# The means' column in a buffer of the "nm" tag: the arrays behind it lie 32 bytes lower in SBUF

## The chip, the cores and the metric

The kernel runs on one core of one Trainium2 chip. The metric is the device time of one execution in microseconds (us); times below are medians over runs unless one run is named.

## What is computed

A decoder trunk of two layers over 256 tokens of width 2048, in float32. Layer 0 mixes with a gated short convolution, layer 1 with multi-head latent attention (16 heads); each layer has a squared-ReLU MLP with 8192 hidden columns, and each of the four sub-layers ends in a DeepNorm LayerNorm.

```python
def sq_relu_mlp(x, w1, w2):
    return jnp.square(jax.nn.relu(x @ w1)) @ w2

for layer in range(DEPTH):                      # DEPTH = 2
    if layer < N_A:                             # layer 0
        mix = short_conv_mixer(h, conv_w_in[layer], conv_w[layer], conv_w_out[layer])
    else:                                       # layer 1
        k_nope, k_pe, v = shared_latent_kv(h, ...)
        mix = mla_mixer(h, ..., k_nope, k_pe, v, cos, sin)
    h = layer_norm(ALPHA * h + mix, ln_g[layer, 0], ln_b[layer, 0])
    h = layer_norm(ALPHA * h + sq_relu_mlp(h, mlp_w1[layer], mlp_w2[layer]),
                   ln_g[layer, 1], ln_b[layer, 1])
```

## The kernel before

Every product is formed from float32 operands that are split into a rounded part ("hi") and the rest ("lo"), so one product takes three matmuls: hi with hi, hi with lo, lo with hi. ScalarE (ACT) casts hi, VectorE (DVE) subtracts to get lo. Weights stream in from HBM as 128x1024 blocks on the SyncE queue (`raw` or `w` tiles), are split into a ring of eight `hi`/`lo` pairs, and are used by TensorE (PE) at once. Activations stay in SBUF.

The work has these stages in order of time: the convolution mixer (products `ps_u`), the first MLP, the latent projections and the attention (`ps_k`, `ps_q`, `ps_v`, `ps_p`, `S`, `tp`, `po`), the output projection (`ps_u` again) and the second MLP. The two MLPs are the larger part of the time. In an MLP, `mlp()` writes out a list of operations with costs and dependencies, and `Work.arrange` places them in one fixed order by a small simulation; the instructions are then issued in that order. In this list two kinds of PE work alternate:

- a *chunk* of the up-projection: 16 matmuls of 512 moving columns (`ps_m<-xhl,hi`), then 16 of 256 (`ps_m<-xhl,lo`);
- a *group* of the down-projection, in a seven-product form for 2x2 blocks: 7 products of three matmuls with 512 moving columns each, summed in the PSUM tiles `sum`. The three matmuls are those of `dot`: the stationary operand is a 128x128 block of the hidden activations (`hc`, `ha`), the moving operand a 512-column half of a weight tile: hi, then lo, then hi again.

Of the seven products of a group the sixth takes its weights from a tile of its own, called `t4`: 128 partitions, its hi part 2048 bytes wide and its lo part behind it. The other six read the ring of `hi`/`lo` tiles.

```python
    FAST = (("1", "11", "11"), ("3", "S4", "22"), ("5", "S1", "T1"), ("6", "S2", "T2"),
            ("2", "12", "21"), ("4", "22", "T4"), ("7", "S3", "T3"))
...
                def fourth():
                    box["f"] = fast.tile([P, 2, BW], F32R, tag="t4", name="t4", bufs=1)
                    scalar.copy(box["f"][:, 0, :], b11())
```

SBUF tiles come from pools, which lie one behind another in each partition: `const`, `act`, `raws`, `whl` (the ring), `tmp`, `small`, and behind these whatever pool is open for a stage: `fast` during an MLP (two `sf` tiles of 4096 bytes and `t4`), `att` and within it `att2` during the attention. `small` holds narrow columns (means, variances, scales); each buffer of a tag takes 32 bytes there. `Norm.means` makes the column `off` (the negative means of the tokens, scaled) at the end of the first MLP; it is read by eight DVE instructions that add up the down-projection's blocks.

In the profile nearly every instruction has the line L71, that of the recording helper, so groups are told apart by the tiles' names. Numbers in names are left out, so `t4` shows as `t`, which is also the name of a 256-column scratch tile; MATMULs on `t` with 512 columns are those on `t4`.

Of the kernel before, what the change touches and what calls it, by code (L numbers as in the profile page):

```python
# [10 lines left out]
F32 = mybir.dt.float32  # L11
# [5 lines left out]
P = 128  # L17
# [36 lines left out]
def trunk(ctx: ExitStack, tc: tile.TileContext, opening, xT, vecs, w_in, w_out, w_kv, w_q, w_uk, w_uv,  # L54
# [32 lines left out]
    small = ctx.enter_context(tc.tile_pool(name="small", bufs=2))  # L87
# [140 lines left out]
    def psum(name):  # L228
        return Banks.next().tile([P, 512], F32, tag="mm", name=name)
# [146 lines left out]
    class Norm:  # L376
# [10 lines left out]
        def means(self):  # L387

            ps = psum("mu0c")
            for t in range(2):  # L390
                tensor.matmul(ps[:, t:t + 1], xres[:, 0, t * P:(t + 1) * P], ones[:, 0:1], start=True, stop=True)
            self.off = small.tile([P, 2], F32, tag="off", name="off", bufs=1)
            vector.tensor_scalar(self.off, ps[:, 0:2], -self.scale, None, ALU.mult)

        def prepare(self, m):
# [1058 lines left out]
```

## Time and profile before

| | |
|---|---|
| median of 3 runs | 1997.64 us (1997.62 to 1998.24) |
| profiled execution: device time | 1998.73 us |
| profiled execution: span, first to last instruction | 1996.9 us |
| TensorE clock granted | 0.998 |
| PE busy | 1983.1 us (99%), 11058 matmuls |
| PE weight loads busy | 1735.0 us (87%) |
| DVE busy | 1752.6 us (88%) |
| ACT busy | 1388.6 us (70%) |
| DMA queue q1, share of 16 engines | 61.5% |
| chain that ended last | PE 98%, DVE 1% |

The profiled execution's span is 1.8 us shorter than its device time, and its device time is 1.1 us above the median of the runs. Rows of groups give: line, engine, operation, written tile `<-` read tiles, shapes, count, busy time in us, mean duration of one in ns, and idle time of the engine ahead of them. A matmul's duration overlaps that of the next one, so the cost of a matmul in a stream is the distance from its start to the next start, which is less than its duration.

### The profile page before, as it was taken

The page shows a single profiled execution, that of the slowest core. Times are in us where ns is not written, and L with a number is a line of the kernel's source. Part 1 is how long each engine was busy: PE and PEld are TensorE (multiplying, and loading weights), DVE is VectorE, ACT ScalarE, POOL GpSimd, SP SyncE. Part 2 cuts the span into 40 slices and gives each one's busy share as a digit, 9 for nine tenths or more (in the row PEclk, how much of TensorE's full clock was granted, in tenths as well). Part 3 has the DMA queues.
Part 4 walks back from the last instruction along what each step waited for, and adds up shares of the span by engine and source line. Part 5 has one row for each costly group of instructions (what it writes and reads, how often), then busy time and mean ns, then how long its engine had stood idle before and what let it go on. Part 6 is the DMA issues. An engine that isn't in the chain of part 4 may idle for free.

```text
span 1996.9 us, 29770 instructions
## 1 busy us (share of the span) xinstructions
PE 1983.1 (99%) x11058; PEld 1735.0 (87%) x11058; DVE 1752.6 (88%) x2630; ACT 1388.6 (70%) x2069; POOL 2.3 (0%) x21
## 2 busy tenths in 40 slices
PE   9999999999999999999999999999999999999997
PEld 8888888988888888888889998898888888888886
DVE  7667667689999999999988888878999999999997
ACT  6444445577887888878856655567788788887871
POOL 0000000000000000000000000000000000000000
PEclk9999999999999999999999999999999999999999
DMA  9755556456666666666765543644666666666673
GB/s 341 230 188 189 191 186 188 156 164 195 208 200 202 205 202 205 200 202 207 221 208 158 165 129 117 204 163 154 201 203 206 200 203 204 202 206 202 199 248 110
DMA packets 107858, 387.39 MB, mean 194 GB/s; under 512 B 11969, under 2 KB 12737, under 8 KB 107713
## 3 DMA queue, kind: packets, MB, share of 16 engines
q1 hardware_dynamic: 107568, 385.36, 61.5%
q8 instruction: 86, 1.41, 0.3%
q14 instruction: 60, 0.48, 0.1%
q10 hardware_dynamic: 144, 0.13, 0.0%
HBM read 383.35 MB, written 2.10 MB: 193 GB/s over the span
## 4 chain that ended last, share of the span: by engine, by line
PE 98%; DVE 1%; issue 0%; ACT 0%; DVEq 0%
PE ps_m L71 31%; PE sum L71 27%; PE ps_u L71 20%; PE ps_d L71 4%; PE ps_w L71 4%; PE ps_g L71 4%; PE ps_q L71 1%; PE ps_v L71 1%; PE S L71 1%; PE ps_k L71 1%; PE ps_wo L71 1%; PE po L71 1%; PE ps_p L71 1%; PE turned L71 0%; DVE lo L71 0%
## 5 line engine op out<-in xcount | busy, mean ns | idle before, releaser
L71 DVE TENSOR_TENSOR lo<-w,hi 128x1024 fp32r<-128x1024 f32 x536 | 640.8, 1220 | 38.5 <-ACT hi L71 37.7
L71 ACT CAST hi<-w 128x1024 fp32r<-128x1024 f32 x536 | 541.8, 1061 | 64.2 <-DVE w L71 63.3
L71 ACT CAST hi<-raw 128x1024 fp32r<-128x1024 f32 x278 | 289.9, 1051 | 252.9 <-PE ps_u L71 155.0
L71 DVE TENSOR_TENSOR lo<-raw,hi 128x1024 fp32r<-128x1024 f32 x278 | 333.8, 1221 | 112.3 <-ACT hi L71 39.7
L71 PE MATMUL ps_m<-xhl,hi 128*128 128x512 f32 x1792 | 425.6, 390 | 0.0
L71 PEld LDWEIGHTS ps_m<-xhl,hi 128*128 128x128 f32 x1792 | 336.1, 188 | 71.7
L71 PE MATMUL sum<-hi,hc 128*128 128x512 f32 x736 | 278.0, 391 | 0.0
L71 PE MATMUL sum<-lo,hc 128*128 128x512 f32 x656 | 257.3, 392 | 0.0
L71 PE MATMUL sum<-hi,ha 128*128 128x512 f32 x640 | 246.5, 389 | 0.0
L71 PEld LDWEIGHTS ps_m<-xhl,lo 128*128 128x128 f32 x1792 | 229.8, 191 | 8.7
L71 PE MATMUL ps_m<-xhl,lo 128*128 128x256 f32 x1792 | 232.5, 283 | 0.0
L71 DVE TENSOR_TENSOR w<-w,w 128x512 f32<-128x512 f32 x312 | 213.7, 685 | 0.3
L71 PE MATMUL ps_u<-xhl_a,hi 128*128 128x512 f32 x704 | 168.1, 391 | 0.0
L71 PEld LDWEIGHTS sum<-hi,hc 128*128 128x128 f32 x736 | 138.6, 188 | 26.7 <-DVE t L71 0.3
L71 PEld LDWEIGHTS ps_u<-xhl_a,hi 128*128 128x128 f32 x704 | 129.4, 188 | 25.1
L71 PEld LDWEIGHTS sum<-hi,ha 128*128 128x128 f32 x640 | 120.2, 188 | 26.2
L71 PEld LDWEIGHTS sum<-lo,hc 128*128 128x128 f32 x656 | 123.6, 188 | 22.3
L71 ACT COPY sums<-sum 128x512 f32<-128x512 f32 x194 | 112.8, 596 | 12.3 <-PE sum L71 11.8
L71 ACT COPY t<-ps_m 128x256 f32<-128x256 f32 x112 | 42.4, 378 | 97.9 <-PE ps_m L71 97.9
L71 ACT COPY sum<-sums 128x512 f32<-128x512 f32 x174 | 105.4, 606 | 0.8
L71 PE MATMUL ps_w<-xd,hi 128*128 128x258 f32 x512 | 94.4, 284 | 0.5 <-DVE xres L71 0.5
L71 PEld LDWEIGHTS ps_u<-xhl_a,lo 128*128 128x128 f32 x704 | 90.3, 191 | 3.4
(201 smaller groups left out, 2785.4 us busy)
## 6 DMA issues: line engine op xcount, KB each, us to landing
w<-in_w_dram SPq DMA_DIRECT2D x224, 512.0 KB, 3.8
w<-in_w2f_dram SPq DMA_DIRECT2D x208, 512.0 KB, 4.3
raw<-in_w_in_dram SPq DMA_DIRECT2D x88, 512.0 KB, 4.5
raw<-in_w_dram SPq DMA_DIRECT2D x64, 512.0 KB, 4.4
raw<-in_w_out_dram SPq DMA_DIRECT2D x32, 512.0 KB, 4.2
raw<-in_w_o_dram SPq DMA_DIRECT2D x32, 512.0 KB, 3.7
raw<-in_w2f_dram SPq DMA_DIRECT2D x16, 512.0 KB, 4.6
row<-in_opening_dram SPq DMA_DIRECT2D x15, 384.0 KB, 5.0
```

Source lines behind the costliest of these rows:

```text
L71: ins = op(*args, **named)
```

## The change

The column `off` had a tag of its own with one buffer. It now takes the next buffer of the tag `nm`, which has two buffers and is otherwise used by the LayerNorm statistics.

```diff
             ps = psum("mu0c")
             for t in range(2):
                 tensor.matmul(ps[:, t:t + 1], xres[:, 0, t * P:(t + 1) * P], ones[:, 0:1], start=True, stop=True)
-            self.off = small.tile([P, 2], F32, tag="off", name="off", bufs=1)
+            self.off = small.tile([P, 2], F32, tag="nm", name="off")
             vector.tensor_scalar(self.off, ps[:, 0:2], -self.scale, None, ALU.mult)
```

In the built programs all five engines have the same instructions in the same order with the same waits; no instruction is added, removed or moved. What differs is where tiles lie. The pool `small` is 32 bytes shorter, so the tags behind `off` in it and the pools opened behind it start 32 bytes lower. Everything up to `tmp` (activations, raw weights, the `hi`/`lo` ring, all of which start at multiples of 128) stays where it was. Start of each tile in its partition, in bytes:

| tile (pool) | before | remainder by 64 | after | remainder by 64 |
|---|---|---|---|---|
| `sf`, two buffers (fast) | 216736, 220832 | 32 | 216704, 220800 | 0 |
| `t4` (fast) | 224928 | 32 | 224896 | 0 |
| `kpe` (att) | 216736 | 32 | 216704 | 0 |
| `rk` (att) | 218816 | 0 | 218784 | 32 |
| `mask_t` (att) | 219904 | 0 | 219872 | 32 |
| `pt`, two buffers (att2) | 221440, 222976 | 0 | 221408, 222944 | 32 |

## The prediction

> **What bounds the kernel now.** I read the page first. Its rows for the span, for PE, and for the chain of waits (by engine, then by line):
>
> ```profile
> span 1996.9 us, 29770 instructions
> PE 1983.1 (99%) x11058; PEld 1735.0 (87%) x11058; DVE 1752.6 (88%) x2630; ACT 1388.6 (70%) x2069; POOL 2.3 (0%) x21
> PE 98%; DVE 1%; issue 0%; ACT 0%; DVEq 0%
> PE ps_m L71 31%; PE sum L71 27%; PE ps_u L71 20%; PE ps_d L71 4%; PE ps_w L71 4%; PE ps_g L71 4%; PE ps_q L71 1%; PE ps_v L71 1%; PE S L71 1%; PE ps_k L71 1%; PE ps_wo L71 1%; PE po L71 1%; PE ps_p L71 1%; PE turned L71 0%; DVE lo L71 0%
> ```
>
> The end is set by the matmul stream itself; most of the chain is `ps_m` and `sum`, the two kinds of MLP work. So a change that moves only addresses can gain or lose in two ways: if a matmul's own spacing depends on where its operands lie, or if DVE becomes so slow that PE waits for it. For the second I read the windows view in the middle of each MLP (busy us and count by engine PE, PEld, DVE, ACT, POOL, then clock and DMA):
>
> ```profile
> 600.00:700.00 100.00, 100.00 (x509) 85.21 (x508) 97.27 (x128) 80.37 (x111) 0.00 (x0) 1.00 0.68 205
> 1600.00:1700.00 100.00, 100.00 (x516) 85.56 (x515) 96.72 (x127) 83.09 (x120) 0.00 (x0) 1.00 0.66 203
> ```
>
> PE never pauses there; DVE has 2.7 to 3.3 us of each 100 to spare.
>
> For the first way I asked which matmuls read a tile that moves. In the MLPs it is `t4` alone (`sf` is read by ACT and DVE only). The view of the tile `sum` gives duration in ns as min/median/max:
>
> ```profile
> L71 PE MATMUL sum<-hi,hc x736: 387/389/504, 411.3 to 1921.5; 128*128 128x512 f32 x184
> L71 PE MATMUL sum<-lo,hc x656: 389/389/402, 411.5 to 1921.7; 128*128 128x512 f32 x164
> L71 PE MATMUL sum<-hi,ha x640: 389/389/397, 445.1 to 1921.9; 128*128 128x512 f32 x160
> L71 PE MATMUL sum<-t,hc x216: 393/397/399, 447.8 to 1921.0; 128*128 128x512 f32 x108
> L71 PE MATMUL sum<-t,ha x96: 397/397/398, 489.8 to 1921.2; 128*128 128x512 f32 x96
> ```
>
> These are matmuls of one shape with stationary operands from the same two arrays. Those whose moving operand lies in the ring take 389 ns; those that read `t4` take 397, with hardly any spread: the fastest `t4` matmul (393) is slower than the median of the others. Now one group in detail. The groups view, first from 704.9 to 707.1 us (products 3 to 5 of this group and the edges), then from 707.1 to 708.3 (the `t4` product and the one behind it; count, busy us and mean ns of one):
>
> ```profile
> L71 PE MATMUL sum<-lo,hc 128*128 128x512 f32 x4 | 1.6, 390 | 0.0
> L71 PE MATMUL sum<-hi,ha 128*128 128x512 f32 x4 | 1.6, 389 | 0.0
> L71 PE MATMUL sum<-hi,hc 128*128 128x512 f32 x3 | 1.2, 389 | 0.0
> ```
>
> ```profile
> L71 PE MATMUL sum<-t,hc 128*128 128x512 f32 x2 | 0.6, 396 | 0.0
> L71 PE MATMUL sum<-t,ha 128*128 128x512 f32 x1 | 0.4, 397 | 0.0
> L71 PE MATMUL sum<-hi,hc 128*128 128x512 f32 x1 | 0.4, 392 | 0.0
> L71 PE MATMUL sum<-lo,hc 128*128 128x512 f32 x1 | 0.4, 398 | 0.0
> L71 PE MATMUL sum<-hi,ha 128*128 128x512 f32 x1 | 0.4, 389 | 0.0
> ```
>
> Behind `t4` the stream does not fall back to 389 at once, although the ring is read again. The next chunk's first two matmuls are still above it (the same view from 708.60 to 708.75, which holds the first, from 708.72 to 708.95, which holds both, and from 709.2 to 711, where it is steady):
>
> ```profile
> L71 PE MATMUL ps_m<-xhl,hi 128*128 128x512 f32 x1 | 0.4, 395 | 0.0
> L71 PE MATMUL ps_m<-xhl,hi 128*128 128x512 f32 x2 | 0.6, 394 | 0.0
> L71 PE MATMUL ps_m<-xhl,hi 128*128 128x512 f32 x9 | 2.2, 389 | 0.0
> ```
>
> The durations overlap, so I look whether the excess is also in the spacing. Timeline of the same group (start, length, what), its first four matmuls and the later ones that I use:
>
> ```profile
> 703.72 0.40 PE L71 MATMUL sum<-hi,hc 128*128 128x512 f32 x1
> 703.95 0.40 PE L71 MATMUL sum<-lo,hc 128*128 128x512 f32 x1
> 704.19 0.39 PE L71 MATMUL sum<-hi,ha 128*128 128x512 f32 x1
> 704.42 0.40 PE L71 MATMUL sum<-hi,hc 128*128 128x512 f32 x1
> ...
> 705.11 0.39 PE L71 MATMUL sum<-hi,hc 128*128 128x512 f32 x1
> ...
> 707.15 0.63 PE L71 MATMUL sum<-t,hc 128*128 128x512 f32 x2
> ...
> 707.85 0.39 PE L71 MATMUL sum<-hi,hc 128*128 128x512 f32 x1
> ...
> 708.54 3.80 PE L71 MATMUL ps_m<-xhl,hi 128*128 128x512 f32 x16
> ```
>
> From 705.11 to 707.15 are nine spacings: 2.04 us, 226.7 ns each. From 707.15 to 708.54 are six: 1.39 us, where six steady ones take 1.36. So the excess is real time on PE, about 30 ns by these rounded starts up to the group's end, and it goes on into the chunk.
>
> **The change part by part.**
>
> *The instructions.* None is added, removed or moved. The column takes the second `nm` buffer, which nothing has used until then; the next norm's statistics go to the first, and only those after the attention come back to this one, long after the column's last reader. Cost: nothing, on both sides.
>
> *`t4`, 32 past a multiple of 64 before, a multiple after.* What sets its matmuls apart from their neighbours? Not shape, order (hi, lo, hi as everywhere) or PSUM. No wait either: the rows above show no idle time, and a wait would scatter where these spread over 6 ns. It is written by an ACT cast and a DVE subtraction as the ring is. What is left is the place: `t4` is the only moving operand of 512 columns that begins 32 past a multiple of 64; all the ring's halves begin at multiples of 128, as `t4` will. I take it that the start within 64 bytes costs the time. The trace shows no such tile at another place, so this is inferred by elimination, not shown.
>
> The price by the rows: the three `t4` matmuls cost 7 + 7 + 8 = 22 ns over 389, the five behind them 3 + 9 + 0 + 6 + 4 = 22 (the 4 is 393, from 394 as the mean of 395 and 393). Together 44 ns a group; with the medians of all groups (three times 8 in the first part) 46. There are (216 + 96) / 3 = 104 such groups, so 104 x 46 ns = 4.8 us. All of it lies on PE, which is 100% busy in these stretches.
>
> Bounds: nothing, if the place is not the cause; 104 x 24 ns = 2.5 us, if only the three reads get cheap and the unrest behind them has another cause; 4.8 us if both go. I take 4.8, since the unrest starts only at `t4` and the nine spacings ahead of it are even.
>
> *Does DVE let PE have it?* PE would run 46 ns faster per group. A group and its chunk are 21 + 32 = 53 matmuls, so 100 us hold 516 / 53 = 9.7 of them, and PE gains 0.45 us in 100. DVE's 2.7 us to spare cover that six times.
>
> *The attention.* `kpe` goes to a multiple of 64, the two `pt` leave it; both are moving operands of unsplit float32 matmuls, 32 of 128 and 32 of 256 columns each. Groups view with shapes kept apart:
>
> ```profile
> L71 PE MATMUL S<-kqva 128*128 128x256 f32 x32 | 9.6, 380 | 0.0
> L71 PE MATMUL S<-kpe,kqva 128*128 128x256 f32 x32 | 9.5, 379 | 0.0
> L71 PE MATMUL S<-kpe,kqva 128*128 128x128 f32 x32 | 6.4, 283 | 0.4 <-DVE kqva L71 0.4
> L71 PE MATMUL S<-kqva 128*128 128x128 f32 x32 | 6.2, 273 | 0.0
> ```
>
> At 256 columns `kpe`, 32 off now, costs no more than the aligned operand (379 against 380); at 128 columns 10 ns more. So `kpe` may win 32 x 10 ns = 0.3 us and `pt` lose as much: net 0. At worst `pt` pays 46 / 3 = 15 ns on 64 matmuls, 1.0 us; at best `kpe` wins 0.6 (64 x 10 ns) and `pt` loses nothing.
>
> *DVE and ACT on the moved tiles.* Operations of one shape, first with the moved tile, then without:
>
> ```profile
> L71 DVE TENSOR_TENSOR t<-w,t 128x512 fp32r<-128x512 f32 x104 | 71.2, 685 | 0.0
> L71 DVE TENSOR_TENSOR w<-w,w 128x512 f32<-128x512 f32 x312 | 213.7, 685 | 0.3
> L71 DVE TENSOR_TENSOR ha<-sf,hc 128x1024 fp32r<-128x1024 f32 x48 | 58.5, 1218 | 0.0
> L71 DVE TENSOR_TENSOR lo<-w,hi 128x1024 fp32r<-128x1024 f32 x536 | 640.8, 1220 | 38.5 <-ACT hi L71 37.7
> L71 DVE TENSOR_TENSOR sf<-ps_m,t 128x256 f32<-128x256 f32 x112 | 46.8, 418 | 0.1
> ```
>
> 685 and 685, 1218 and 1220: DVE does not notice the place. `rk` and `mask_t`, which lose their multiple of 64, are read by DVE only. I put all this at nothing.
>
> *The sum.* The profiled execution took 1998.73 us with a span of 1996.9; less 4.8 they would be 1993.9 and 1992.1. The median of the runs is 1.1 us lower than the profiled time, so the forecast is 1997.64 - 4.8 = 1992.8 us, 0.24% less.
>
> **The rivals.** I call a change of over 0.2% (4.0 us) faster or slower, about what a measurement of this kernel can tell from no change.
>
> *No change: the place is not the cause.* Then 397 belongs to something that stays with `t4`, such as being read soon after it is written, and the time stays at 1997.6. For it: the trace has no second tile to compare, and `kpe` at the same remainder costs nothing at 256 columns. Against it: `kpe` is read by unsplit matmuls, which take 380 ns for half the columns, so a slower fetch could hide behind the slower columns; and freshness should make a wait or scatter, and there is neither. [...] Chance 0.16.
>
> *Half: the reads get cheap, the unrest stays,* or PE meets an operation that comes a little later than it does: 1997.64 - 2.5 = 1995.1. Against it: the even spacings ahead of `t4`. For it: the group's first matmuls start 230 to 240 ns apart too (703.72 to 704.42), with no `t4` near, behind 256-column matmuls. Chance 0.08.
>
> *Slower: DVE pays for the new place.* Once `sf` and `t4` start at the same remainder as the ring and the raw weights, DVE instructions that read two such tiles might collide. About 1,070 us (104 groups at 9.7 in 100 us) hold at least 71.2 + 58.5 + 46.8 = 176 us of DVE work on these tiles, and 3% of 1,070, or 32 us, to spare. PE starts to wait when that work grows by 32 / 176 = 18%; at 21% and no gain from `t4` the time is 1997.6 + 5 = 2002.6. Against it: `lo<-w,hi` reads two tiles at multiples of 128 already, at 1220 ns. Chance 0.04, with the other cases that end over 4.0 us slower.
>
> **How the numbers follow.** The forecast keeps 0.72: 1992.8, between 1991.8 (4.8 and the 0.6 of `kpe` gained, and 0.4 to 0.6 by which runs differ) and 1993.8 (`pt` at its worst). The half case lies at 1995.1 and with the same spread ends at 1995.6. From 1991.8 to 1995.6 are 0.72 + 0.08 = 0.80, which is the range; no change (0.16) and slower (0.04) are left out. Faster by over 4.0 us is the forecast without its weak edge, 0.71; within 0.2% are no change, the half case and that edge, 0.25; slower 0.04.
>
> **What would show it.** Right: all `sum<-t` matmuls at 389 instead of 397, the two `sum` matmuls behind them and the next chunk's first two at 389; the group from its first start to the chunk's first start 4.82 us before (703.72 to 708.54), 4.78 after; span 1992.1. The unrest in the first two products stays, as the ring does not move. Half: `sum<-t` near 389 but 398 behind it. Wrong: `sum<-t` still 397 at the new place, then the place was never the cause; or `sum<-t` at 389 and the span unchanged, with idle time of PE ahead of `hi` or `lo` in the MLP windows. A `po<-pt` row 10 ns or more longer would show the price at the attention.

## The result and the profile after

The changed kernel takes 1993.77 us (median of 13 runs, 1993.14 to 1994.14) against 1998.06 us for the kernel before in the same comparisons: ratio 0.9978, 95% interval 0.9971 to 0.9986, so 4.3 us or 0.22% faster. Forecast were 1992.8 us and 0.24%. The profiled execution's span went from 1996.9 to 1991.9 us. The page of the changed kernel, its rows for the span and the engines:

```profile
span 1991.9 us, 29770 instructions
PE 1978.0 (99%) x11058; PEld 1734.5 (87%) x11058; DVE 1752.0 (88%) x2630; ACT 1388.2 (70%) x2069; POOL 2.3 (0%) x21
```

PE is busy 5.1 us less, DVE and ACT by less than 1 us: the gain is in the matmul stream. The view of the tile `sum` (duration ns min/median/max):

```profile
L71 PE MATMUL sum<-hi,hc x736: 389/389/501, 410.7 to 1916.4; 128*128 128x512 f32 x184
L71 PE MATMUL sum<-lo,hc x656: 389/389/398, 410.9 to 1916.7; 128*128 128x512 f32 x164
L71 PE MATMUL sum<-hi,ha x640: 389/389/397, 444.4 to 1916.9; 128*128 128x512 f32 x160
L71 PE MATMUL sum<-t,hc x216: 389/389/389, 447.1 to 1916.0; 128*128 128x512 f32 x108
L71 PE MATMUL sum<-t,ha x96: 388/389/389, 488.9 to 1916.2; 128*128 128x512 f32 x96
```

The matmuls on `t4` are at 389 ns like the rest, where they were at 397. The timeline of the group that was shown before, now from 702.17:

```profile
702.17 0.40 PE L71 MATMUL sum<-hi,hc 128*128 128x512 f32 x1
...
705.60 0.61 PE L71 MATMUL sum<-t,hc 128*128 128x512 f32 x2
...
706.96 3.79 PE L71 MATMUL ps_m<-xhl,hi 128*128 128x512 f32 x16
710.58 1.60 PE L71 MATMUL ps_m<-xhl,lo 128*128 128x256 f32 x12
```

From `t4` to the next chunk are 1.36 us for six spacings, 226.7 ns each; before it was 1.39. The unrest behind `t4` is gone with its cause. The group takes 4.79 us from its first start to the chunk's, against 4.82.

One thing is new. In the waits of PE's weight loads a row stands that the kernel before did not have (us in total, times, longest):

```profile
PEld sum L71 <- ACT sum L71: 0.8, 2, 0.4
```

Once in each MLP a weight load now waits for ACT, 0.4 us each time, which copies a stored sum back into PSUM.

To compare kernels below I work out two numbers from each trace's matmul starts, over the 104 groups: by how much the spacings of the three `t4` matmuls exceed three times 226.7 ns, and the same for the eight matmuls behind them. Before these were 22 and 25 ns, now 0 and 0 in the median group. Where a text below says "shift", it means how many bytes further, modulo 256, the moving operand starts than the weights of the same matmul.

### The profile page after: what moved, and what is told of

Same layout as the page of the kernel before. It is cut to its first block, busy times and chain, and to the rows that moved or that the text cites. A ratio compares the mean times of both kernels' runs of the same rounds, so it can differ in the third digit from the quotient of the medians.

```text
span 1991.9 us, 29770 instructions
## 1 busy us (share of the span) xinstructions
PE 1978.0 (99%) x11058; PEld 1734.5 (87%) x11058; DVE 1752.0 (88%) x2630; ACT 1388.2 (70%) x2069; POOL 2.3 (0%) x21
## 4 chain that ended last, share of the span: by engine, by line
PE 98%; DVE 1%; issue 0%; ACT 0%; DVEq 0%
PE ps_m L71 31%; PE sum L71 27%; PE ps_u L71 20%; PE ps_d L71 4%; PE ps_w L71 4%; PE ps_g L71 4%; PE ps_q L71 1%; PE ps_v L71 1%; PE S L71 1%; PE ps_k L71 1%; PE ps_wo L71 1%; PE po L71 1%; PE ps_p L71 1%; PE turned L71 0%; DVE lo L71 0%
## 5 line engine op out<-in xcount | busy, mean ns | idle before, releaser
L71 ACT ACTIVATE sf<-sf 128x512 f32<-128x512 f32 x120 | 76.6, 638 | 27.4 <-DVE sf L71 27.3
```

Of the source, the lines that this page charges most:

```text
L71: ins = op(*args, **named)
```

## The experiments

**Is it `t4` alone, and is it the multiple of 64?** Two kernels move `t4` and nothing else, one from the kernel before, one from the changed one:

```diff
-                    box["f"] = fast.tile([P, 2, BW], F32R, tag="t4", name="t4", bufs=1)
+                    box["f"] = fast.tile([P, 2 * BW + 32], F32R, tag="t4", name="t4", bufs=1)[:, 8:8 + 2 * BW].rearrange("p (v c) -> p v c", v=2)
```

> The kernel before with t4 alone begun 32 bytes later (224960, a multiple of 64 but not of 128); sf, kpe, pt and all else stay where they were. Theory (the start of t4 within 64 bytes costs the time): all t4 matmuls at 389 ns, the two sum matmuls and two ps_m matmuls behind them at 389, time 4.3 us below the kernel before, as the change had. Rival (another moved tile brings the gain, sf or those of the attention): t4 matmuls may get cheap but the time stays within 1 us of before. Rival (a multiple of 128 is needed): t4 matmuls stay at 397 and the time at that of before.

> The changed kernel with t4 alone put back to 224928 (32 past a multiple of 64); sf and the attention's tiles stay at their new places. Theory: t4 matmuls at 397 again, the unrest behind them back, time equal to the kernel before within 0.5 us. Rival (another moved tile brings the gain): time stays within 1 us of the changed kernel, 4.3 us below before.

With `t4` put back to its old place in the changed kernel: 1997.74 us against 1997.72 before (ratio 1.0, 0.9991 to 1.0009). So the whole gain is `t4`'s; `sf` and the attention's tiles give nothing that can be seen (0.02 us between the two). But `t4` at 224960, a multiple of 64, made the kernel before slower: 2000.4 us (ratio 1.0014, 1.0005 to 1.0023). The view of `sum`, its `t4` rows, first for `t4` put back, then for `t4` at 224960:

```profile
L71 PE MATMUL sum<-t,hc x216: 393/397/399, 447.4 to 1920.8; 128*128 128x512 f32 x108
L71 PE MATMUL sum<-t,ha x96: 397/397/397, 489.4 to 1921.1; 128*128 128x512 f32 x96
```

```profile
L71 PE MATMUL sum<-t,hc x216: 394/397/398, 446.8 to 1922.6; 128*128 128x512 f32 x108
L71 PE MATMUL sum<-t,ha x96: 394/394/394, 488.8 to 1922.8; 128*128 128x512 f32 x96
```

The `t4` matmuls themselves cost about the same (397 ns at the old place, 394 to 397 at 224960); the unrest behind them grew from 25 to 50 ns and reaches the tenth matmul behind (the eight counted above hold 40 of the 50). Over 104 groups that is the measured 2.7 us. The rule that the prediction inferred, a start within 64 bytes, is wrong.

**Which places are free?** From the changed kernel, `t4` at other offsets, a different one in each MLP (the first number in the slice above becomes `16 if idx == 1 else 4` and so on, in elements of four bytes):

> The changed kernel with t4 at 64 past a multiple of 128 in the first MLP and at 16 past it in the second. Theory (2048 bytes that begin inside a stretch of 64 bytes touch 33 such stretches instead of 32): first MLP 389 ns, second MLP 397, as at 32. Rival (stretches of 128 bytes): 397 in both. Rival (only an odd multiple of 32 costs): 389 in both. Rival (lines of 16 bytes): 389 in both, since 16 is a line's start.

> The changed kernel with t4 at 4 bytes past a multiple of 64 in the first MLP and at 48 past it in the second. Theory (stretches of 64 bytes): 397 ns in both, however small the shift. Rival (only an odd multiple of 32 costs): 389 in both. Rival (lines of 16 bytes): above 389 at 4, 389 at 48. Rival (cost grows with the shift): 4 nearer to 389, 48 above 397.

The two kernels took 1999.79 and 1999.35 us (one run each). Every one of these places costs, and not in the order of a growing shift: in the table below 16 costs the least in the product itself (10 ns) and 4 the most (29 ns). The theory falls with 64 (23 ns where it had none), whole lines of 16 bytes with 16 (10 ns, and 40 behind it); of the rivals that of 128 bytes is left. I then noticed that in the changed kernel the operands of `ps_m`, `ps_u` and `sum`, moving or stationary, all start 128 past a multiple of 256, which left two theories: a moving operand must begin at such a multiple itself (A), or it must lie where the weights lie that are loaded beside it (B). Four kernels for that:

```text
 e5: hi part of t4 at its place and lo part 32 bytes off in the first MLP; hi part 32 and lo part 64 bytes off in the second
 e6 (from the kernel before):  + shim pool of 32 bytes ahead of the ring's pool
 e7 (from the changed kernel): + shim pool of 32 bytes ahead of the pool act
 e8: t4 at +128 bytes in the first MLP, +256 in the second
```

The shim is one small tile that is cleared once. In e6 what lies behind the ring moves with it, so `t4` goes to 64. In the second MLP of e5 the kernel is not what was meant: its lo slice begins at element `BW + 16` of the tile, so the lo part did not stay at its place but went to a shift of 64.

> The changed kernel with t4's two parts placed apart: in the first MLP the hi part (read by matmuls 1 and 3 of the product) at its changed place and the lo part (matmul 2) 32 bytes further, in the second MLP hi 32 bytes further and lo at its changed place. The theory of 64-byte stretches has fallen (t4 at 64 past a multiple of 128 cost more than at 32). If each read pays for its own place: first MLP about 9 ns in matmul 2 alone and 389 ns in 1 and 3; second MLP 9 ns each in 1 and 3. If a read off the others' place disturbs a rhythm between the moving reads and the weight loads beside them: spacings above 227 ns go on for five or more matmuls behind a single odd read, so the first MLP's group loses 20 ns or more for one read.

> The kernel before with 32 bytes put in ahead of the ring of hi and lo tiles, so the ring begins 32 past a multiple of 128 and t4 at 64 past; activations (xhl, hc, ha, z) stay at multiples of 128. Theory A (a moving operand must itself begin at a multiple of 128): every sum matmul with a moving operand in the ring pays about 7 ns (some 2,500 with those of ps_d and ps_v, 18 us), ps_m, whose moving operand is xhl and whose weights are the ring, stays at 389; time about 2016. Theory B (what counts is where the moving operand lies relative to the weights that are loaded beside it): ps_m and ps_u pay too, some 5,500 matmuls of 512 columns at 7 ns, 38 us; time about 2036.

> The changed kernel with 32 bytes put in ahead of all activations, raw weights, ring and fast tiles: every operand of every large matmul lies 32 past a multiple of 128, and all of them keep their places relative to each other. Theory A (absolute start): all 5,900 matmuls of 512 columns pay about 7 ns, 41 us, and those of 256 columns up to as much; time 2035 to 2060. Theory B (relative places): nothing changes, sum, ps_m and t4 matmuls at 389, time within 0.5 us of the changed kernel, 1993.8.

> The changed kernel with t4 128 bytes further in the first MLP and 256 bytes further in the second (everything else, and with it the weights hc and ha, at 128 past a multiple of 512, as t4 was in the changed kernel). If what counts is the place modulo 128: 389 ns in both. Modulo 256: above 389 in the first, 389 in the second. Modulo 512: above 389 in both.

With everything 32 bytes off, but together, the time is 1993.82 us (ratio to before 0.9979, 0.997 to 0.9989), that of the changed kernel. With the ring and what lies behind it 32 bytes off against the activations it is 2020.75 us (ratio 1.0114, 1.0097 to 1.0131). Groups view with shapes kept apart, two of the wide rows for everything together, then for the ring's kernel:

```profile
L71 PE MATMUL ps_m<-xhl,hi 128*128 128x512 f32 x1792 | 424.6, 390 | 0.0
L71 PE MATMUL ps_u<-z,hi 128*128 128x512 f32 x256 | 61.2, 391 | 0.0
```

```profile
L71 PE MATMUL ps_m<-xhl,hi 128*128 128x512 f32 x1792 | 437.0, 396 | 0.0
L71 PE MATMUL ps_u<-z,hi 128*128 128x512 f32 x256 | 62.3, 396 | 0.0
```

In the ring's kernel the moving operands of `ps_m` (`xhl`) lie where they always did; only their weights moved, and their wide matmuls still pay 6 ns. So A is out: with everything moved together no operand's own place cost anything (1993.82 us against 1993.77), and with the ring and what lies behind it moved against the activations 22.8 us were lost (2020.75 against 1998.0), so what counts here is where the moving operand lies relative to the weights. (B's size, 38 us, was too large: the narrow matmuls of `ps_m` and `ps_u` became 1 to 3 ns cheaper at this shift, 280 to 282 by duration against 283, and the first five wide ones of a `ps_u` chunk had been dear already, spaced by 233, 236, 228, 232 and 231 ns in the kernel before.) The trace of `t4` at +128 and +256, groups view over the first MLP, then over the second:

```profile
L71 PE MATMUL sum<-t,hc 128*128 128x512 f32 x108 | 33.2, 391 | 0.0
L71 PE MATMUL sum<-t,ha 128*128 128x512 f32 x48 | 19.1, 398 | 0.0
```

```profile
L71 PE MATMUL sum<-t,hc 128*128 128x512 f32 x105 | 32.1, 389 | 0.0
L71 PE MATMUL sum<-t,ha 128*128 128x512 f32 x48 | 18.7, 389 | 0.0
```

At 256 bytes it is free again (389 ns), at 128 not (391 and 398). The kernels e5 and e8 took 1997.08 and 1995.58 us (one run each). All places of `t4` together, as its shift against the weights `hc` and `ha` modulo 256, with the excess worked out from the starts (median or mean of about 52 groups each):

| shift of `t4`, bytes | three `t4` matmuls, ns | the eight behind, ns | kernel |
|---|---|---|---|
| 0 (also +256) | 0 | 0 | changed, e8 |
| 4 | 29 | 38 | e4 |
| 16 | 10 | 40 | e3 |
| 32 | 22 | 25 | before, e2 |
| 48 | 20 | 36 | e4 |
| 64 | 23 | 40 | e1, e3 |
| 128 | 16 | 25 | e8 |
| hi 0, lo 32 | 15 | 38 | e5 |
| hi 32, lo 64 | 21 | 2 | e5 |

At 16 and 64 the unrest goes on past the eight, to 50 ns in all, and at 48 to 40. Summed over the 16 spacings from `t4` on, the excess of all groups is 4.84 us before and 7.57 in e1, 6.88 in e3, 6.53 in e4, 3.94 in e5 and 2.39 in e8; the differences from before are those of the measured times within 0.1 us, in the kernels with one run too.

One odd read (lo alone at 32) unsettles the stream for ten matmuls, its own included, and costs 53 ns; three odd reads (32, 64, 32) cost 21 and leave 2 ns behind. So what is lost is not a fixed price for each read. That spacings above 227 ns go on behind a single odd read is what e5 was to tell; the rhythm between moving reads and weight loads, from which its expectation derived this, was the author's guess and is not shown.

**Does the shift set a steady spacing?** In a chunk all wide and narrow matmuls have one shift. Two kernels give five stages shifts of their own, by starting the arrays `xhl_a`, `z`, `xhl` and `oT` some bytes into their room:

```diff
-        t = act.tile([P, ROOM[tag] // 4], dtype, tag=tag, name=name)[:, :n]
+        t = act.tile([P, ROOM[tag] // 4], dtype, tag=tag, name=name)[:, at // 4:at // 4 + n]
```

> The changed kernel with the moving operands of five stages shifted against the weights that are loaded beside them, by a number of bytes of its own in each: the convolution's inputs 64 (ps_u from xhl_a), its outputs z 96, the first MLP's xhl 128, the attention's output oT 160, the second MLP's xhl 192. Theory B (place relative to the weights, modulo 256): each of these 512-column matmuls is spaced by more than the 226.7 ns at 0, by 4 to 9 ns; at 128 the cost of t4 at 128 (about 8 ns at first) stays for the whole chunk; in all some 3,850 matmuls by about 7 ns, 27 us. Rival (a moving operand pays only when it differs from the moving operand ahead of it): no cost inside a chunk at any shift, since all its reads are shifted alike, and the time stays within 2 us of the changed kernel. If a shift gives less than 226.7 ns, a kernel faster than the changed one is at hand.

> The same with other shifts: xhl_a 16, z 224, the first MLP's xhl 4, oT 32, the second MLP's xhl 240. Theory B: oT at 32 and z at 224 (32 to the other side) near the 233.5 ns that a shift of the ring by 32 gave; 4, 16 and 240 tell how near to 0 the place must be: if whole lines of 16 bytes count, 4 costs nothing and 16 something; if every byte counts, 4 costs too. Rival as before: no cost inside a chunk at any shift.

They took 1997.79 and 2013.01 us (one run each). From the starts, mean spacing in the settled part of a chunk and the whole chunk of 32 matmuls:

| stage | shift, bytes | wide, ns | narrow, ns | chunk, ns |
|---|---|---|---|---|
| `ps_u` (`xhl_a`) | 0 | 227 | 120 | 5571 |
| `ps_u` (`xhl_a`) | 16 | 232 | 117 | 5576 |
| `ps_u` (`xhl_a`) | 64 | 229 | 113 or 118, by turns | 5519 |
| `ps_u` (`oT`) | 32 | 233 | 117 | 5600 |
| `ps_u` (`z`) | 96 | 233 | 120 | 5653 |
| `ps_u` (`oT`) | 160 | 234 | 119 | 5640 |
| `ps_u` (`z`) | 224 | 233 | 118 | 5627 |
| `ps_m` | 0 | 227 | 120 | 5541 |
| `ps_m` | 4 | 240 | 124 | 5797 |
| `ps_m` | 128 | 233 | 119 | 5626 |
| `ps_m` | 192 | 233 | 113 | 5558 |
| `ps_m` | 240 | 233 | 117 | 5612 |

The groups view over the first MLP shows the extreme, first with `ps_m` at 0 (changed kernel), then at 4 (second of the two kernels):

```profile
L71 PE MATMUL ps_m<-xhl,hi 128*128 128x512 f32 x857 | 203.1, 389 | 0.0
```

```profile
L71 PE MATMUL ps_m<-xhl,hi 128*128 128x512 f32 x832 | 207.8, 401 | 0.0
```

The shift costs inside chunks where all moving reads are shifted alike (wide matmuls at 229 to 240 ns against 227), so the rival falls: it is not the step from one moving operand to the next. `z` at 224, 32 bytes below its weights, gives 5627 ns; the ring 32 bytes above `z` gave 5627 too, although there the weights moved. Of the shifts tried zero is best for the wide matmuls (227 ns), but not for the narrow ones (120 ns, against 113 at 192), and at 64 the whole chunk of `ps_u` is 52 ns shorter than at zero. That is also why the first of the two kernels lies only 4 us above the changed one instead of 27: from the starts, its shifted wide matmuls cost 14 us more in all, its narrow ones 9 us less. In the second, the shift of 4 alone makes 56 chunks x 256 ns = 14 us. The chunks of the convolution at 64 take turns between 5490 and 5543 ns, with narrow matmuls at 113 and at 118.

**A version that beats both.** First I tried to give each kind its best shift: the lo weights, which only narrow matmuls of these chunks load, were moved alone (64 bytes, or 192 in the later stages; the rope tables went to the attention's pool for room).

> The changed kernel with the lo weight tiles alone moved against the moving operands, in the products of 16 wide and 16 narrow matmuls only (ps_u and ps_m): the narrow matmuls (256 columns) read the lo weights, the wide ones (512) the hi weights, which stay at 0. The lo weights lie 64 bytes further in the convolution and the first MLP, 192 bytes further in the output projection and the second MLP; in all other products they stay at 0. Room comes from the rope tables, which move into the attention's pool. Theory B, with the shifts' measured spacings: wide matmuls keep 226.7 ns, narrow ones go from 120 to 113 or 114, about 16 x 6 = 96 ns a chunk; some 185 chunks, less what the change of place costs at each turn between wide and narrow (0 to 25 ns): time 13 to 18 us below the changed kernel, 1976 to 1981. Rival (the spacing depends on the place of the moving operand alone, as a shift of it moved it against everything): narrow matmuls stay at 120 and the time at 1993.8. If DVE, at 97% in the MLPs, cannot keep up with a PE that is 1% faster, PE waits ahead of hi and lo and less is gained.

It takes 1991.05 us (ratio to before 0.9966, 0.9954 to 0.9978), 2.7 us less than the changed kernel instead of 13 to 18: the narrow matmuls settle at 118 ns, not at 113, and the groups of the second MLP, which come behind them, take 35 ns more each. With the shift alone their spacing is not given: behind wide matmuls at 0 they settle at 118 ns, behind wide ones at their own shift of 64 or 192 they had 113, in the convolution by turns with 118. So the last kernel takes the shift of 64 as it was measured, for moving operands of wide and narrow matmuls together, in all five stages (`at=64` in the lines above):

> The changed kernel with the moving operands of ps_u and ps_m (xhl_a, z, the two MLPs' xhl, oT) 64 bytes further, weights where they were: the shift that gave the convolution's chunks 5519 ns instead of 5571 (16 wide matmuls at 229.5 ns, 16 narrow at 115). Theory B: the same chunk in all five stages; 73 chunks of ps_u gain 52 ns each (3.8 us), 112 chunks of ps_m between 22 ns (5541 before, 5519) and 50 ns (with the unrest ahead of them), 2.5 to 5.6 us: time 1984.4 to 1987.5. Rival (the gain belongs to the convolution's place in time or to its arrays): ps_m stays near 5541 ns a chunk and the time at 1991 to 1994.

It takes 1985.23 us, ratio to before 0.9936 (0.9923 to 0.995): 0.64% less than the kernel before, 8.5 us less than the changed one, inside what was expected. Groups view over the first MLP (440 to 985 us) of this kernel, then of the kernel before:

```profile
L71 PE MATMUL ps_m<-xhl,hi 128*128 128x512 f32 x864 | 207.6, 392 | 0.0
L71 PE MATMUL ps_m<-xhl,lo 128*128 128x256 f32 x855 | 106.0, 276 | 0.0
L71 PE MATMUL sum<-t,hc 128*128 128x512 f32 x108 | 32.9, 389 | 0.0
```

```profile
L71 PE MATMUL ps_m<-xhl,hi 128*128 128x512 f32 x850 | 202.0, 390 | 0.0
L71 PE MATMUL ps_m<-xhl,lo 128*128 128x256 f32 x848 | 110.0, 283 | 0.0
L71 PE MATMUL sum<-t,hc 128*128 128x512 f32 x108 | 33.6, 396 | 0.0
```

By duration wide matmuls are 2 ns dearer, narrow ones 7 ns cheaper. By the distance of their starts, against the changed kernel, wide ones of `ps_m` are 3.3 ns dearer and narrow ones 5.9 cheaper, so a chunk takes 5499 ns instead of 5541: 112 of them make 4.7 us, and 73 of `ps_u` at about 50 ns 3.7 us, together 8.4 of the 8.5 us.

## Why the prediction was right, and where not

*Which matmuls pay, and how much.* Right. The excess of 22 ns in the `t4` product and of 22 to 25 behind it vanished: from the starts, the eight spacings from `t4` on held 4.85 us above 226.7 ns each over all groups before, as the sum had it, and 0.58 us after.

*Both parts go together.* Right, and `t4` put back brings both back (22 and 25 ns). The half rival's first clause, an unrest with another cause, is out.

*DVE lets PE have it.* Right for DVE, which stays at 97.6 and 96.5 us of each 100 in the middle of the MLPs, but the sum lacked a term. In two groups PE waits for ACT's copy into PSUM, the row of waits shown above; in the first the spacings behind `t4` are 390 and 336 ns where 227 is normal, in the second 383 and 339, 0.27 us each. That is 0.5 of the 0.58 us left, the half rival's second clause, and takes 4.8 to the measured 4.3 us. That the faster stream brings these waits on is not shown: the kernel with `t4` put back, as slow as before, has one of 0.5 us in its trace. The forecast's 1992.8 was low by that and by the kernel before running at 1998.06 in the later runs. The span of 1991.9 (1992.1 forecast) agrees better than it should, since the first `sum` matmul already starts 0.6 us earlier (410.7 against 411.3), ahead of any `t4`.

*DVE and ACT on the moved tiles.* Right. ACT's 120 activations of `sf` take 638 ns, 640 before, and its casts from `sf` of 1024 columns 1066, 1068 before. DVE in the groups view after:

```profile
L71 DVE TENSOR_TENSOR t<-w,t 128x512 fp32r<-128x512 f32 x104 | 71.0, 683 | 0.0
L71 DVE TENSOR_TENSOR ha<-sf,hc 128x1024 fp32r<-128x1024 f32 x48 | 58.4, 1217 | 0.0
L71 DVE TENSOR_TENSOR sf<-ps_m,t 128x256 f32<-128x256 f32 x112 | 46.6, 416 | 0.4 <-ACT t L71 0.2
```

*The attention.* Net nothing, as said, but by another way. Neither `kpe` gained its 10 ns nor `pt` lost them; rows after:

```profile
L71 PE MATMUL S<-kpe,kqva 128*128 128x128 f32 x32 | 6.5, 283 | 0.4 <-DVE kqva L71 0.4
L71 PE MATMUL po<-pt,kqva 128*128 128x128 f32 x32 | 6.1, 274 | 0.0
```

283 is what `kpe` had before, so those 10 ns are not the place's; 274 is what `pt` had before.

*The mechanism.* The step that failed, with no harm to the number, is "the start within 64 bytes costs the time". The runs show in its place: what counts is the shift between the moving operand and the weights, modulo 256 as far as `t4` at +128 (16 and 25 ns) and +256 (0 and 0) tells. The place 224896 was free because it lies where `hc` and `ha` lie modulo 256, not because it is a multiple of 64. The price was read rightly off the rows; that the new place would be a free one was luck as far as the rule goes. Had the column's tag been 32 bytes longer instead of absent, `t4` would have gone to 224960, a multiple of 64 too, and the forecast by the same rule would have had the wrong sign: that place cost 2.7 us.

The elimination had named the right tile; it could not name the right property, because every other moving operand of 512 columns had a shift of 0, with the same remainder by 64, 128 and 256 as its weights. The trace before did hold other shifts, where the prediction did not look: the 258-column matmuls of `ps_w` and `ps_g` move parts of `xd` that lie 1032 bytes apart, so by the addresses of the built program their shifts go through all multiples of 8. Averaged by shift, these 1200 matmuls are spaced mostly by 118 (shift 48) to 124 ns (24), and the changed kernel repeats nearly the same values. Position in the stream is mixed into this, so it is a hint and no proof.

*The rivals.* "The place is not the cause" fell with `t4` put back (1997.74 us, its matmuls at 397 ns). DVE paying for the new place fell with the rows above.

What in the chip makes the shift cost time is not shown. The runs show its size: in the ring's kernel 32 bytes between the moving operand and the weights cost the wide `ps_m` matmuls 6 ns by duration, 390 to 396. Whole lines of 16 bytes do not explain it in either form that the expectations gave them: a shift of 16, free in that of e3, costs a wide matmul 5 ns (227 to 232), and one of 4, free in that of e10, 13 ns (227 to 240). Whether a matmul's own weights count or the next ones, which are loaded beside it (weight loads are busy for 1734.5 of the 1991.9 us, matmuls for 1978.0), is not shown either: in most of the stages compared here both lie alike.

## What to carry to other kernels

In a stream bound by matmuls, look at the distance between starts, by position in the loop: here a tile whose matmuls took 397 ns where their twins took 389, without scatter and without a wait, differed from them by where it lies, and 25 of the 47 ns that it cost were paid by the matmuls behind it. What mattered was the place of the moving operand relative to the weights, with 256 bytes as free as none (389 ns), so a small column in front of big arrays was worth 4.3 us, 32 bytes ahead of the ring cost 22.8, and a shift of all arrays together did nothing (1993.82 us against 1993.77). Since the best shift was not zero for all shapes (narrow matmuls 113 ns at 192, 120 at 0) and a shift worked only together with the stream it was measured in (118 ns instead of 113 with the lo weights moved alone), try it on the chip, array by array, and keep what the starts show.

## What had not been expected of the hardware

- The settled spacing of 512-column matmuls with split operands went from 226.7 ns at shift 0 to 240 ns at 4 bytes, and that of 256-column ones from 113 ns (192 bytes) to 124 ns (4 bytes).
- A single read with another shift unsettled ten matmuls: one lo read 32 bytes off cost 53 ns, its own spacing and those behind it together.
- The first five wide matmuls behind narrow ones pay 27 ns together in the kernel before, in the same pattern of spacings (233, 236, 228, 232, 231) as the last of the unrest behind `t4` (236, 228, 232, 231). With a shift of 64 in the chunks it stays for the groups (25 ns).
- One shift has more than one settled spacing: at 64 bytes the narrow matmuls settle at 113 or at 118 ns. In the last kernel the chunks of `ps_u` take turns between the two, and of the 112 chunks of `ps_m` 106 settle at 113. What decides between them stays open.
